# A hybrid encoder layer on one core: transfers in pieces and staged later, copies moved to GpSimd, q's norms from transposes

## The chip, the cores and the metric

The kernel is one program on one core of a Trainium2 chip. Its time is the device time from launch to end in microseconds (us). Every instruction belongs to an engine with its own in-order queue: PE is TensorE (matmuls and transposes; PEld its weight loads), DVE is VectorE, ACT is ScalarE, POOL is GpSimd, SP is SyncE, from whose queue all DMA transfers of this kernel are issued. An engine that waits for a semaphore holds up all that stands behind the waiting instruction in its own queue.

## The reference

One encoder layer over two sequences (1024 and 2048 tokens, model width 1024): an RMSNorm, one input projection, two parallel token mixers, a gated merge, an output projection and a residual. Branch A is neighbourhood attention with 8 heads of 64. Branch B is a bidirectional gated DeltaNet with 4 heads of 128, which is where most of the change sits. Cut to what matters here:

```python
proj = einsum('btd,de->bte', _rms_norm(x, norm_g), w_in)
qkv = silu(conv5(qkv_b)).reshape(B, T, 3, 4, 128)         # centred 5-tap conv
q = _l2_norm(qkv[:, :, 0]) * 128 ** -0.5                  # x * rsqrt(sum(x * x) + EPS)
k = _l2_norm(qkv[:, :, 1]);  v = qkv[:, :, 2]
# per direction, in chunks: a triangular solve, then a scan that carries S
sol = triangular_solve(a_mat, rhs, lower=True, unit_diagonal=True)
o_b = _rms_norm(o_fwd + o_bwd, dn_norm_g) * silu(z_b)
merged = sigmoid(gate_a) * (o_a @ w_branch_a) + sigmoid(gate_b) * (o_b @ w_branch_b)
y = x + merged @ w_out
```

## The kernel before

All float32 operands of the large products are split into a high and a low float16 part, and a product is three float16 matmuls (high by high, high by low, low by high).

**Stage 1, the function `deltanet`, from the start to about 1705 us.** The tokens stand in 12 half blocks of 256. The normalised input of each half block, transposed and split (`hh`, `hl`, 512 KB each), is written once to DRAM (`hdr`) and then fetched again for each of five rounds over the weights; there are two buffers of each, so half n is fetched when half n-2 has been let go. The projection's weights come in tiles of 1024x128 (`w`). For each tile, half a tile at a time (256 KB, `wst`, in the functions `staged`, `maximum` and `split_tile`), DVE takes the largest magnitude, a scale is made of it, and after a second fetch ACT and DVE make the high and the low part. Two such streams of weights run side by side, and the buffer `xt` has two places, one for each.

The order is written out by hand, in slots. `step_slot` issues one slot: it lets the generators of the chains (S), the inverses (I), the weights and rows (W, H), the operands (O) and the finishing steps (F) each go one step, and between these it fills PE with products of weights and halves until the slot holds 33.5 units (one unit is a float16 matmul of 256 columns). A generator that yields n is called again n slots on. `at(n, ...)` puts a call at the start of the n-th slot from now, `end(...)` at the end of this slot, after three quarters of its products. All five queues of this stage keep the order in which the code issued them. If the products run dry, transposes of the identity (`idle`) fill a slot to half.

The weights' steps stand in the middle of a slot:

```python
st = staged(src, k)          # DMA of a half tile
yield WD                     # WD = 1
amax(wm2[:, n, k:k + 1], st) # DVE
yield
```

So a half tile is issued in the middle of one slot, read by DVE in the middle of the next, and the next half tile is issued one slot later. `launch`, at a slot's start, fetches a half block with two transfers and hands it to the products two slots later.

For each head and each block of 512 tokens (24 in all) `operands` makes q, k and v from the convolution. q's norm: ACT squares q into the spent raw tile, PE multiplies the four squared 128x128 pieces by a column of ones (`pn`, float32, 8 columns), and DVE and POOL make the reciprocal root. `inverse` (12 in all) solves the triangular systems in 32x32 blocks: the blocks' inverses come back as `RR`, are copied into the diagonal of `P` (`u.E`, half of them by ACT, half by DVE) and, in `level1`, into the tile `Q64`, all of 32 partitions by 128 elements.

**Stage 2, to about 2384 us,** is the attention: slots of four tokens' tiles of projection (`ppn`) with the scores, the softmax and the values of earlier blocks. There PE, DVE and ACT keep the written order; DMAs and POOL are ordered by the framework's scheduler. Near its end `begin` starts a *chunk* (256 tokens of the merge): it loads `x` in two halves, attention's result `oad` and DeltaNet's `obd`, then `z` and the gates `th`; POOL multiplies `obd` by `z`, DVE takes the largest magnitude of `x`. `begin` takes six numbers: how many slots on the loads, the product on POOL and the four other steps come. `oad` of block 5 is written only shortly before by `block_out`.

**Stage 3** is the merge and the output projection.

## Time and profile before

| | |
|---|---|
| median of 3 runs | 2824.47 us (2822.04 to 2829.65) |
| the profiled execution | 2828.49 us, span 2826.7 us |
| mean granted clock of TensorE | 0.989 |
| busy: PE / DVE / ACT / POOL | 2705.9 / 1771.9 / 1398.1 / 899.6 us |

A row of the timeline or of the groups names the engine, the operation, `out<-in` by the program's tiles, the shape and how many; a bracket or the part behind the bar gives the time for which the engine stood idle just before, and what ended the wait. The granted clock is given as a share of 2.4 GHz: 1.00 is 2.4 GHz, 0.50 is 1.2 GHz. Matmuls overlap, so that a matmul's own duration is longer than its step: what it costs PE is the distance from its start to the next one's.

### The profile page before, as it was taken

How to read it: one execution, taken by the hardware profiler on the slowest of the kernel's cores; microseconds unless marked ns; L12 is line 12 of the kernel's file. 1: busy time of each engine (PE TensorE's matmuls, PEld its weight loads, DVE VectorE, ACT ScalarE, POOL GpSimd, SP SyncE). 2: the span in 40 equal slices, each digit the busy share in tenths (PEclk: the TensorE clock that was granted, in tenths of full speed). 3: DMA queues.
4: the chain of work that ended last, by engine and by line, in shares of the span. 5: the costliest groups of instructions: out<-in, count | busy, mean ns of one | idle time of the engine just before them, and what ended most of it. 6: DMA issues, size and time to landing. Idle time of an engine off the chain costs nothing. (4 is left out here: it accounts for less than half of the span.)

```text
span 2826.7 us, 65273 instructions
## 1 busy us (share of the span) xinstructions
PE 2705.9 (96%) x25140; PEld 2165.2 (77%) x25140; DVE 1771.9 (63%) x4266; ACT 1398.1 (49%) x3861; POOL 899.6 (32%) x1545
## 2 busy tenths in 40 slices
PE   7999999999999999999999999999999989999999
PEld 6888888978788977888888896666666657766675
DVE  7667766576675767747576522666666667555554
ACT  4455554555445555456454543666666755112211
POOL 2232120131112221112212215444444443555553
PEclk9999999999999999999999999999999999999999
DMA  8433442344533354322436737433332465443341
GB/s 255 152 112 94 122 116 81 105 139 124 125 99 99 112 145 119 90 88 88 131 103 172 201 118 209 132 105 95 94 102 86 140 200 204 165 164 130 134 147 68
DMA packets 488277, 365.00 MB, mean 129 GB/s; under 512 B 144291, under 2 KB 450847, under 8 KB 487071
## 3 DMA queue, kind: packets, MB, share of 16 engines
q1 hardware_dynamic: 487967, 360.84, 42.9%
q8 instruction: 198, 3.24, 0.5%
q14 instruction: 112, 0.92, 0.1%
HBM read 262.53 MB, written 98.20 MB: 128 GB/s over the span
## 5 line engine op out<-in xcount | busy, mean ns | idle before, releaser
L61 PE MATMUL pp<-hh,w 128*128 128x256 f16 x6912 | 1196.4, 275 | 8.7 <-DVE thz L61 3.9
L61 PEld LDWEIGHTS <-w 128*128 128x128 f16 x10368 | 1014.9, 99 | 135.1 <-issue 5.2
L61 PE MATMUL pp<-hl,w 128*128 128x256 f16 x3456 | 948.9, 275 | 0.6 <-DVE hl L61 0.6
L61 PEld LDWEIGHTS <-y 128*128 128x128 f16 x2304 | 224.8, 98 | 37.6 <-issue 9.4
L61 PE MATMUL ppn<-whi,rl 128*128 128x384 f16 x768 | 252.2, 328 | 0.0
L61 PE MATMUL ppn<-whi,rh 128*128 128x384 f16 x768 | 251.2, 327 | 0.0
L61 PE MATMUL ppn<-wlo,rh 128*128 128x384 f16 x768 | 251.2, 327 | 0.0
L61 POOL TENSOR_TENSOR th<-th 128x128 f32<-128x128 f32 (+1 forms) x240 | 153.8, 657 | 142.0 <-DVE th L61 129.2
L61 PEld LDWEIGHTS <-rh 128*128 128x128 f16 x1536 | 144.9, 98 | 69.6 <-issue 1.0
L61 ACT ACTIVATE thz<-pp,wfc 128x256 f32<-128x256 f32 x288 | 124.6, 472 | 148.5 <-PE pp L61 91.7
L61 PEld LDWEIGHTS <-mm 128*128 128x128 f16 x1008 | 98.7, 98 | 115.1
L61 ACT ACTIVATE mm<-th 128x256 f16<-128x256 f32 x144 | 59.1, 447 | 236.1 <-POOL th L61 231.8
L61 DVE TENSOR_TENSOR pl<-pT,ph 128x384 f16<-128x384 f32 (+1 forms) x192 | 110.9, 600 | 82.3 <-ACT ph L61 81.0
L61 DVE CUSTOM_DVE_ANT_0 Sb<-pS,bt 128x384 f32<-128x384 f32 (+1 forms) x192 | 108.9, 599 | 70.9 <-PE pS L61 30.6
L61 POOL TENSOR_TENSOR rqk<-rqk,mhalf 128x4 f32<-128x4 f32 x48 | 52.7, 1097 | 298.4 <-DVE rqk L61 295.1
L61 ACT ACTIVATE Sb<-Sb,nm,pq 128x384 f32<-128x384 f32 (+1 forms) x192 | 140.2, 734 | 0.7 <-DVE nm L61 0.7
L61 DVE TENSOR_REDUCE wm<-wst 128x1 f32<-128x512 f32 (+1 forms) x111 | 82.2, 762 | 79.0 <-DMA wst<-in_w_in 60.3
L61 ACT ACTIVATE vn<-pk,nbeg 128x128 f32<-128x128 f32 x176 | 64.8, 368 | 134.7 <-PE pk L61 133.9
L61 ACT ACTIVATE raw<-pp,wfc 128x256 f32<-128x256 f32 x144 | 63.6, 474 | 137.2 <-PE pp L61 135.2
L61 ACT ACTIVATE Os<-pon,rsn 128x64 f32<-128x64 f32 x192 | 49.9, 312 | 156.3 <-PE pon L61 156.2
L61 DVE SCALAR_TENSOR_TENSOR mm<-th,mm 128x256 f16<-128x256 f32 x144 | 80.6, 592 | 66.1 <-ACT mm L61 65.9
L61 PEld LDWEIGHTS <-rl 128*128 128x128 f16 x768 | 75.2, 98 | 60.1 <-issue 30.9
(621 smaller groups left out, 5614.6 us busy)
## 6 DMA issues: line engine op xcount, KB each, us to landing
wst<-in_w_in SPq DMA_DIRECT2D x124, 256.0 KB
gtd<-thz SPq DMA_DIRECT2D x192, 128.0 KB
hh<-hdr SPq DMA_DIRECT2D x48, 512.0 KB
hl<-hdr SPq DMA_DIRECT2D x48, 512.0 KB
th<-gtd SPq DMA_DIRECT2D x24, 1024.0 KB
vw<-vd SPq DMA_DIRECT2D x320, 64.0 KB
IT<-gd SPq DMA_DIRECT2D x48, 256.0 KB
bt<-ud SPq DMA_DIRECT2D x256, 48.0 KB
```

Of the source, the lines that this page charges most:

```text
L61: i = f(*a, **k)
```

## The change

Eight edits: (1) a half block is fetched in four transfers of 256 KB, one now, two in the next slot, one in the slot after, and handed over four slots later instead of two; (2) `WD` is 2 instead of 1, the half tiles of weights are issued at the end of the slot (`end`) and the trailing yields of `maximum` and `split_tile` are gone, so that a half tile still comes every second slot; (3) the steps that load the decay rows wait one slot more; (4) q's norm: PE transposes q (`ptq`), ACT squares the transposed tile out of PSUM, DVE sums over 128 elements; (5) 192 copies of 32x128 (half of `u.E`'s and all of `Q64`'s) go from DVE to POOL; (6) 28 identity transposes stand in the prologue; (7) a chunk loads `obd` and `z` ahead of `oad`; (8) the first chunk's `begin` stands one slot earlier, with its later steps in the same slots as before.

```diff
--- before.py
+++ after.py
@@ -265,7 +265,7 @@
             t.n = n
         wsc, wfc = (dcp.tile([128, NT + 5], F32, name=n) for n in ("wsc", "wfc"))
         wm2 = dcp.tile([128, NT + 20, 2], F32, name="wm2")
-        WD = 1
+        WD = 2
 
 
         c1 = dcp.tile([128, 8], F32, name="c1")
@@ -431,14 +431,13 @@
 
             n = src.shape[0] // 256
             st = wk.tile([128, n, src.shape[1]], F32, name="wst", tag="xt", bufs=2)
-            SY.dma_start(st, src[128 * n * k:128 * n * k + 128 * n].rearrange("(k p) c -> p k c", p=128))
+            end(SY.dma_start, st, src[128 * n * k:128 * n * k + 128 * n].rearrange("(k p) c -> p k c", p=128))
             return st
 
         def maximum(src, n, k):
             st = staged(src, k)
             yield WD
             amax(wm2[:, n, k:k + 1], st)
-            yield
 
         def split_tile(t, old, k):
 
@@ -455,7 +454,6 @@
             t.half += 1
             if t.half == 2:
                 at(1, setattr, t, "w", t.w_)
-            yield
 
 
         wba = [dcp.tile([128, 8, 16], F16, name=f"wba{i}") for i in range(2)]
@@ -603,7 +601,7 @@
                 for j, (a, b) in enumerate(((0, 1), (0, 0), (1, 0), (1, 1))):
                     r0, c0 = 256 * p + 128 * a, 512 * b + 128 * q
                     SY.dma_start(st[:, j], w_out[0][r0:r0 + 128, c0:c0 + 128])
-                yield 1 + WD
+                yield 2
                 hi, lo = (wk.tile([128, 7, 128], F16, name="wos", tag=t, bufs=2) for t in ("raw0", "raw2"))
                 S.activation(hi[:, 0:3], st[:, 1:4], AF.Identity, scale=so4)
                 end(low, lo[:, 0:3], st[:, 1:4], hi[:, 0:3])
@@ -870,7 +868,7 @@
                     yield
                 for d in range(2):
                     SY.dma_start(DT[:, d], tb.gd[4 * bi:4 * bi + 4, 4 * d + h, :][None, :, :].to_broadcast([128, 4, 128]))
-                yield 2
+                yield 3
                 for d in range(2):
                     G.tensor_tensor(DT[:, d], DT[:, d], mask[:, d, None, :].to_broadcast([128, 4, 128]), op=ADD)
                 yield
@@ -924,14 +922,15 @@
                 T.transpose(pt[:, c, :], o.kh[:, c, :], ident)
             S.activation(o.KQ[:, :, 0, :], pt, AF.Copy)
             cv.more(4)
-            S.activation(flat(rqt), qv, AF.Square)
-            yield
-            pn = ps_tr.tile([128, 4, 8], F32, name="pn", tag="tr")
+            yield
+            ptq = ps_tr.tile([128, 4, 128], F32, name="ptq", tag="tr")
             for c in range(4):
-                T.matmul(pn[:, c, :], flat(rqt)[:, c, :], ones, start=True, stop=True)
+                T.transpose(ptq[:, c, :], qv[:, c, :], ident)
             nq = wk.tile([128, 4], F32, name="rqk", bufs=4)
+            S.activation(flat(rqt), ptq, AF.Square)
             cv.silu()
-            end(rsq, nq, pn[:, :, 0])
+            end(V.tensor_reduce, nq, flat(rqt), AX.X, ADD)
+            end(rsq, nq, nq)
             done(0)
             yield
             G.tensor_scalar(o.rq, nq, 128.0 ** -0.5, 1.0, op0=MUL, op1=MUL)
@@ -1082,7 +1081,7 @@
                         if b % 2:
                             S.activation(u.E[sl(b), :, sl(b)], u.Pd[sl(b)], AF.Copy)
                         else:
-                            V.tensor_copy(u.E[sl(b), :, sl(b)], u.Pd[sl(b)])
+                            G.tensor_copy(u.E[sl(b), :, sl(b)], u.Pd[sl(b)])
             yield
 
             def level1(l, lv, Z):
@@ -1094,8 +1093,8 @@
 
                 for u in l:
                     ca, cb = 32 * u.qa - u.A, 32 * u.qb - u.A
-                    V.tensor_copy(Q64[sl(u.qa), :, ca:ca + 32], u.Qd[sl(u.qa)])
-                    V.tensor_copy(Q64[sl(u.qb), :, cb:cb + 32], u.Qd[sl(u.qb)])
+                    G.tensor_copy(Q64[sl(u.qa), :, ca:ca + 32], u.Qd[sl(u.qa)])
+                    G.tensor_copy(Q64[sl(u.qb), :, cb:cb + 32], u.Qd[sl(u.qb)])
 
             def level2(l, lv, Z):
                 for c in range(4):
@@ -1249,8 +1248,13 @@
                 n = l.pop(0)
                 t = half_tiles()
                 for i in range(2):
-                    SY.dma_start(t[i], hdr[n % 12 // 2][:, i, n % 2])
-                at(2, halves.__setitem__, n, t)
+                    for j in range(2):
+                        f = SY.dma_start, t[i][:, 4 * j:4 * j + 4], hdr[n % 12 // 2][:, i, n % 2, 4 * j:4 * j + 4]
+                        if i + j:
+                            at(i + j, *f)
+                        else:
+                            f[0](*f[1:])
+                at(4, halves.__setitem__, n, t)
             l = todo["op"]
             if l and len(live) < SLOTS and len(gens["H"]) + len(ahead) + len(live) < 6 + (len(rel) > 11) and opstage[0] and nraw.get(l[0], 0) == (6 if l[0][1] in LAST else 9) and \
                     len(tabs) > l[0][1] // 2:
@@ -1299,6 +1303,10 @@
         two(pt0[0], pt0[0].st)
         pts.append(transposed(xs[1], t0[0], 128))
         low_part(pts[1], *t0, 128)
+
+        t = ps_tr.tile([128, 4, 128], F32, name="idle", tag="tr")
+        for _ in range(28):
+            T.transpose(t[:, 0, :], ident, ident)
         sg = small()
         next(sg)
         amax(wm2[:, 1, 0:1], pt0[1].st)
@@ -1694,7 +1702,7 @@
             c.th = [big(f"th{h}", 4, 2, TB) for h in range(2)]
             op = big("op", 2, 2, 4, TB)
             c.o = [(op[:, j, 0], op[:, j, 1]) for j in range(2)]
-            for t, d in ((x[:, 0], oad), (x[:, 1], obd), (z, szd)):
+            for t, d in ((x[:, 1], obd), (z, szd), (x[:, 0], oad)):
                 SY.dma_start(t, d[i // 2].rearrange("(k p) t -> p k t", p=128)[:, :, cs])
             for h in range(2):
                 SY.dma_start(c.th[h].rearrange("p e j t -> p (e j) t"), gtd[i][8 * h:8 * h + 8].rearrange("e p t -> p e t"))
@@ -1926,8 +1934,8 @@
             if hp_ == 3 and b == 0:
                 branch_weights(0)
             for t in range(4):
-                if hp_ == 3 and b == 2 and t == 2:
-                    begin(order[0], (0, 3, 3, 4, 4, 5))
+                if hp_ == 3 and b == 2 and t == 1:
+                    begin(order[0], (0, 4, 4, 5, 5, 6))
                 mm = proj_mm(w, b, t)
                 slot(mm)
                 work(1, mm)
```

The order on SP around the fetch of one half block late in round two, before (`wst` are half tiles of weights, `hh` and `hl` the half block, `IT<-gd` the decay rows, `gtd`, `szd` and `zad` stores):

```order
370 L61 DMA ed_13745<-P 32x4x32 x8
371 L61 DMA IT<-gd_2717 128x4x128 x2
372 L61 DMA gtd_98<-thz 128x256
373 L61 DMA wst<-in_w_in 128x4x128 x2
374 L61 DMA gtd_98<-thz 128x256 x2
375 L61 DMA hh<-hdr_70 128x2048
376 L61 DMA hl<-hdr_70 128x2048
377 L61 DMA wst<-in_w_in 128x4x128 x2
```

The same half block on SP in the change:

```order
411 L61 DMA hh<-hdr_70 128x1024
412 L61 DMA hl<-hdr_70 128x1024
413 L61 DMA ed_13908<-P 32x4x32 x8
414 L61 DMA gtd_98<-thz 128x256
415 L61 DMA wst<-in_w_in 128x4x128 x2
416 L61 DMA hl<-hdr_70 128x1024
417 L61 DMA wst<-in_w_in 128x4x128 x2
418 L61 DMA gtd_98<-thz 128x256 x2
419 L61 DMA hh<-hdr_70 128x1024 x2
420 L61 DMA hl<-hdr_70 128x1024
421 L61 DMA wst<-in_w_in 128x4x128 x2
422 L61 DMA hl<-hdr_70 128x1024
```

The four pieces of a half block now stand apart, with half tiles of weights between them.

On DVE, the start of one inverse in the order before (`RR` are the blocks' inverses, `wm` the maxima of half tiles):

```order
1222 L61 STREAM_TRANSPOSE RR<-RR 128x512
1223 L61 COPY P<-RR 32x4x32 x8
1224 L61 TENSOR_REDUCE wm_141<-wst 128x1 x2
1225 L61 COPY Q_147<-RR 32x4x32 x4
1226 L61 SCALAR_TENSOR_TENSOR P<-raw_12664,cw,P 128x512
```

On POOL in the change, where such copies stand now, between the convolution's adds and the decay rows' adds (`IT<-IT,mask`):

```order
383 L61 COPY P<-RR 32x4x32 x8
384 L61 COPY Q_147<-RR 32x4x32 x4
385 L61 TENSOR_TENSOR Vt<-Vt,KQ 128x512
386 L61 TENSOR_TENSOR P<-P,KQ 128x512
387 L61 TENSOR_TENSOR IT<-IT,mask 128x512 x2
388 L61 COPY Q_147<-RR 32x4x32 x4
```

The twelve copies of the first half of an inverse have left DVE's queue and stand in POOL's; the four of the second half come behind the adds that wait for the decay rows.

On SP at the first chunk, before (`oad<-otn` is the write of attention's block 5, `vd` and `vw` attention's values):

```order
940 L61 DMA oad_23559<-otn 128x512
941 L61 DMA vw<-vd_28329 128x1x256 x3
942 L61 DMA vd_28329<-vt 128x256
943 L61 DMA x<-oad_23559 128x4x256
944 L61 DMA x<-obd_76 128x4x256
945 L61 DMA wst<-in_w_branch_b 128x4x128
946 L61 DMA z<-szd_88 128x4x256
947 L61 DMA th_33103<-gtd_99 128x8x256
```

And in the change:

```order
1005 L61 DMA x<-obd_76 128x4x256
1006 L61 DMA z<-szd_88 128x4x256
1007 L61 DMA th_33134<-gtd_99 128x8x256
1008 L61 DMA oad_23702<-otn 128x512
1009 L61 DMA wst<-in_w_branch_a 128x4x128
1010 L61 DMA th_33135<-gtd_99 128x8x256
1011 L61 DMA x<-oad_23702 128x4x256
```

`obd` and `z` now stand ahead of the write of `oad`, and only the load of `oad` stands behind it.

## Rows read from the trace of the kernel before

**Rows 1.** The page: busy time, share of the span and instructions of each engine.
```profile
PE 2705.9 (96%) x25140; PEld 2165.2 (77%) x25140; DVE 1771.9 (63%) x4266; ACT 1398.1 (49%) x3861; POOL 899.6 (32%) x1545
```

**Rows 2.** Windows, stages 1 and 2: width, each engine's busy time, clock, DMA share, GB/s.
```profile
30.00:1681.00 1651.00, 1577.97 (x16423) 1402.12 (x16422) 1080.49 (x2527) 860.41 (x2455) 347.39 (x602) 0.99 0.43 123
1706.00:2384.00 678.00, 653.19 (x5418) 435.36 (x5417) 428.16 (x1313) 433.38 (x1193) 317.12 (x637) 0.99 0.44 128
```

**Rows 3.** Waits of PE, then of DVE, in stage 1: us in total, times, longest.
```profile
PE lv L61 <- DVE Z L61: 11.2, 5, 4.9
...
DVE X L61 <- DMA YT<-ed: 30.6, 7, 7.0
```

**Rows 4.** Groups of DVE by shape: busy, mean ns, idle before and by whom.
```profile
L61 DVE TENSOR_REDUCE wm<-wst 128x1 f32<-128x512 f32 x94 | 61.7, 681 | 67.8 <-DMA wst<-in_w_in 49.2 <-DMA wst<-in_w_out 11.5 <-DMA wst<-in_w_branch_b 5.4
...
L61 DVE COPY Q<-RR 32x128 f32<-32x128 f32 x96 | 22.7, 236 | 1.5
```

**Rows 5.** Timeline, 997 to 1008 us, SP, DVE and PE: start, duration, instruction.
```profile
997.72 0.97 SPq L61 DMA_DIRECT2D wst<-in_w_in  x2
...
1001.53 0.66 SPq L61 DMA_DIRECT2D hh<-hdr  x1
...
1004.16 1.47 DVE L61 TENSOR_REDUCE wm<-wst 128x1 f32<-128x512 f32 x2 [6.04 <-DMA wst<-in_w_in]
...
1006.22 0.41 DVE L61 COPY Z<-lv 128x256 f32<-128x256 f32 x1
...
1006.78 1.12 PE L61 MATMUL lv<-P,Z 64*64 64x64 f32 x16 [4.85 <-DVE Z L61]
```

**Rows 6.** Timeline of PE: first and last of ten such waits.
```profile
477.10 0.39 PE L61 MATMUL lv<-P,Z 64*64 64x64 f32 x6 [2.10 <-DVE Z L61]
...
1376.75 0.51 PE L61 MATMUL pm<-ident,wma 128*128 128x128 f32 x3 [1.75 <-DVE wma L61]
```

**Rows 7.** Windows: five half-clock stretches of stage 1, the largest, then all five.
```profile
1005.21:1012.03 6.82, 5.25 (x36) 4.10 (x37) 6.72 (x16) 4.03 (x17) 1.11 (x2) 0.50 0.69 222
...
sum 20.43, PE 18.52 PEld 13.41 DVE 19.28 ACT 13.55 POOL 1.34; mean PE 3.71 PEld 2.68 DVE 3.86 ACT 2.71 POOL 0.27
```

**Rows 8.** Timeline of PE around q's sums and around a group of four transposes.
```profile
595.71 0.96 PE L61 MATMUL pn<-ones,raw 128*128 128x8 f32 x8
596.52 0.27 PE L61 MATMUL pp<-hh,w 128*128 128x256 f16 x1
...
603.87 0.63 PE L61 MATMUL ptv<-ident,P 128*128 128x128 f32 x4
604.34 0.27 PE L61 MATMUL pp<-hh,w 128*128 128x256 f16 x1
```

**Rows 9.** Timeline, 2258 to 2276 us: SP, POOL and PE at the first chunk.
```profile
2258.13 0.45 SPq L61 DMA_DIRECT2D oad<-otn  x1
...
2261.72 0.38 SPq L61 DMA_DIRECT2D x<-oad  x1
...
2263.24 0.50 SPq L61 DMA_DIRECT2D z<-szd  x1
...
2270.95 2.35 POOL L61 TENSOR_TENSOR x<-x,z 128x1024 f32<-128x1024 f32 x1 [6.69 <-DMA z<-szd]
...
2275.86 0.69 PE L61 MATMUL pqk<-ident,sqn 128*128 128x128 f32 x2 [5.99 <-POOL sqn L61]
```

**Rows 10.** Windows: the half-clock stretch at the first chunk.
```profile
2274.97:2281.79 6.82, 5.93 (x22) 2.56 (x23) 2.59 (x8) 0.75 (x2) 3.32 (x8) 0.50 0.34 99
```

**Rows 11.** Groups of POOL: a small copy, and the decay rows' adds.
```profile
L61 POOL COPY raw<-raw 128x2 f32<-128x2 f32 x96 | 17.5, 217 | 172.2 <-ACT raw L61 171.7
...
L61 POOL TENSOR_TENSOR IT<-IT,mask 128x512 f32<-128x512 f32 x48 | 60.9, 1284 | 75.0 <-DMA IT<-gd 69.9 <-PE idle L61 5.2
```

**Rows 12.** One tile's instructions: the copies into `Q64`, ns shortest/median/longest.
```profile
L61 DVE COPY Q<-RR x96: 204/218/1157, 268.4 to 1584.8; 32x128 f32<-32x128 f32 x96
```

**Rows 13.** Timeline of PE in the prologue, where the 28 transposes go.
```profile
20.25 0.47 PE L61 MATMUL pm<-ident,wma 128*128 128x128 f32 x1 [3.59 <-DVE wma L61]
```

## The prediction

> **What bounds the kernel now.** I read the page's busy times first: PE is busy for 2705.9 of 2826.7 us [rows 1], so the end moves by only two things, less work on PE or less waiting of PE. The windows by stage come next. In stage 1 PE is busy for 1577.97 of 1651 us, in stage 2 for 653.19 of 678 [rows 2]: 73 and 25 us stand open, and the merge behind has nearly nothing. Then the waits of PE, to see for whom it waits. In stage 1 the largest is for DVE's copy `Z`, 11.2 us in five waits [rows 3], though DVE is busy for only 1080 of 1651 us [rows 2]. So DVE is not too slow, it is late, and the groups of DVE tell why: before the maxima of half tiles of weights it stood idle for 67.8 us, 66 of these for the transfer `wst` [rows 4].
>
> One such chain, read forward in the timeline [rows 5]: SP issues two half tiles at 997.72; they land at 1004.16, 6.4 us later, with a half block of 1 MB (`hh`, `hl`) issued into them at 1001.53; DVE has nothing else it may do and waits 6.04 us; the copy `Z`, three instructions behind in its queue, comes at 1006.22; PE's `lv<-P,Z` needs it and had stood still for 4.85 us. I find ten waits of PE behind a late `wst` of this kind, from 477.10 us to 1376.75 us [rows 6], together 22 us. After five of them the records show PE's clock at 0.50, that is 1.2 GHz, for 20.43 us, in which PE was busy for 18.52 [rows 7]; at 2.4 GHz that work is done in half, so 9.3 us more belong to the same cause.
>
> **The change part by part.** *q's norm.* The step from the start of `pn` to the next matmul is 595.71 to 596.52, 0.81 us for four products; four transposes take 603.87 to 604.34, 0.47 us [rows 8]. There are 24 operand blocks: 24 x 0.34 = 8.2 us less work on PE, and all of it on the bounding engine. DVE gets 24 sums over 512 elements; the nearest row, a reduction of the same size, is 681 ns [rows 4]: 16 us on an engine with a third of stage 1 free. ACT's square is the same size as before, but it now stands behind PE's transposes of its own slot, and the tanh and the exponentials behind it wait with it; PE's own waits for ACT are small, so I put this with the new waits below.
>
> *The weights' transfers.* A unit on PE is about 0.12 us (0.47 / 4) [rows 8], a slot of 33.5 units 3.9 us. Before, a half tile is issued in the middle of one slot and read in the middle of the next: 3.9 us, less than the 6.4 us of rows 5. Now it is issued after three quarters of a slot and read in the middle of the second slot after: 1.75 slots, 6.9 us, 2.9 us more lead. Of the ten waits (the longest 4.85, 3.22 and 2.65) that leaves 1.95 and 0.3 us and takes 19.7 of 22 away, if each shrinks by the lead. The pieces of the half block act in the same direction, since the 1 MB that ran into rows 5 now comes as 256 KB, 512 KB and 256 KB in three slots. Against it stands that SP issues in order and may itself be late. Bounds: nothing, and all of 31.3 us (22 + 9.3). I take 0.7 of it, 22 us: the lead alone gives 0.9 of the waits, and I leave a fifth for late issues and for clock stretches that another wait brings on.
>
> *The first chunk.* SP may load `oad` only after its write, issued at 2258.13; the load goes out at 2261.72 and `z` behind it at 2263.24; POOL, in order, stands for `z` until 2270.95, and the norms of the projection stand behind that product on POOL, so PE waits 5.99 us for `sqn` [rows 9]. The clock is then at 0.50 for 6.82 us, 5.93 of them busy [rows 10]: 3.0 us. In the change `obd` and `z` are issued ahead of the write of `oad` and one slot earlier, so they have landed when POOL comes to them; the load of `oad` alone is late, and only DVE's maximum reads it, two slots on. I take the whole, 9.0 us; what is late next there is that maximum, with room. At the least it gives 4, if 2 MB of `z`, `obd` and `th` delay the write of `oad` and the values' loads behind it.
>
> *The copies.* Two kinds of 96, of one size, at 0.236 us [rows 4]: 45 us leave DVE, and with them the odd long one (median 218 ns, longest 1157) [rows 12]. On POOL the trace has no such copy. Its copy of 2 elements takes 0.217 us, its add of 512 elements 1.284 us [rows 11], so 192 cost 42 to 247 us; I take the lower end's neighbourhood, 0.3 us and 58 us, and POOL is busy for only 347 of 1651 us [rows 2]. What hides them: PE reads `Q64` two slots after the copies are issued (7.8 us) and the diagonal of `P` three slots after. Gone is that cover where POOL stands before the adds of the decay rows, for which it waited 69.9 us in all [rows 11]; the extra slot of edit 3 gives those 3.9 us more. The Trainium skill, GPSIMD Engine Reference, section 4.1, says that elementwise work belongs on VectorE and that GpSimd is about twice as slow with two inputs and near par with one; no row here shows a copy of this size on POOL. By the factor of two a copy takes 0.47 us, and the sum would be the same while POOL's free time hides it.
>
> *The prologue.* PE stands 3.59 us for a maximum at 20.25 [rows 13]; 28 transposes at 0.12 us are 3.3 us and fit into it at 2.4 GHz, and at 1.2 GHz hold the next product up by 3 us. Behind it PE waits for the next weights from DVE anyway. From 3 lost to 3 won; I take 1 won.
>
> *New waits.* ACT behind PE, POOL's queue, and slots in which the products run dry because a half block is handed over two slots later: a half block carries eight tiles of 24 matmuls, 192 x 0.12 = 23 us, against four slots of 15.6 us, so this holds except in the last rounds, where four tiles last 11.5 us. Between 0 and 14 us; I take 4.
>
> **The sum.** 8.2 + 22 + 9.0 + 1 - 4 = 36 us. The profiled execution took 2828.5 us, 2792.5 after; the median of the runs lies 4 us under it, so I forecast 2788 us. Its own bounds: all of the weights' 31.3, 3 from the prologue, no new waits and 5 from shorter waits for the inverses' transfers give 2768; a quarter of the weights' part, 4 from the chunk and 14 of new waits give about 2816.
>
> **The rivals.**
> *Another transfer takes the place.* DVE also waits 30.6 us for `X<-YT`, the inverses' blocks [rows 3], and that lead is not changed. If a DVE freed of one wait only meets the next, the weights' part gives 6 instead of 22: 2804. For it: the two lie near each other in the same queue. Against it: the ten waits of rows 6 follow `wst`, not these.
> *It does not do what it says.* With two places for two streams, a half tile's buffer is read by DVE in the very slot at whose end the next transfer is issued into it. If DVE is late, SP stands for it and holds stores and half blocks behind. Then the longer lead gives nothing and SP's hold costs some 5: 8 + 9 + 1 - 4 - 5 = 9 us, 2815.
> *POOL becomes what PE waits for.* The copies of an inverse's second half stand behind the decay rows' adds. If PE waits 2 us in each of 12 inverses, and half of these bring a half-clock stretch that costs 1.9 us (9.3 / 5), 35 us go: 2823. For it is the 69.9 us of rows 11, against it the two slots of cover. The Trainium skill's section named above speaks for this one; no row shows its price.
> *Slower: the half blocks come late.* There are two buffers, and half n is fetched only when half n-2 is let go. If its last piece, which SP issues two slots later than before and behind the weights, lands after the products want it, PE waits, say 1 us, and loses 1.9 us to the clock: 2.9 us for each half block. 44.5 us (the 36 and 8.5 more) are reached at 16 of the 48; at 24 it is 70 us, 2858. Against it: 23 us of products against 15.6 us.
>
> **How the numbers follow.** I give 0.60 to the forecast, 0.20 to the other transfer, 0.08 to the lead that gives nothing, 0.07 to POOL, 0.05 to the half blocks. The range is 2770 to 2814: it holds the forecast's own bounds but for their ends, and the first rival; the rest lies above. A measurement of this kernel can tell about 0.3%, 8.5 us, from no change, so faster means under 2816. Faster: 0.86 (the forecast, nearly all of the first rival, half of the second); the same: 0.09 (POOL, the other half); slower: 0.05.
>
> **What would show it.** The steps are right if DVE's idle time before `wm<-wst` falls from 67.8 to under 25 us, the half-clock stretches of stage 1 become fewer, PE shows no wait for `sqn` near the first chunk and POOL none for `z` there, and the step of `ptq` is 0.44 to 0.5 us. Wrong would be: `wst` waits as long as before, PE waits for `hl` or `hh` by DMA, or waits of `lv` for POOL. If PE's idle time in stage 1 stays near 73 us, the forecast fails with it.

## The result and the profile after

The changed kernel takes 2801.16 us (median of 4 runs, 2797.34 to 2805.1) beside 2824.16 us of the kernel before in the same session: ratio 0.9916, interval 0.9895 to 0.9936. That is 23 us less, inside the range of 2770 to 2814 us, and 13 us above the forecast of 2788. The profiled execution took 2802.75 us with a span of 2801.0, 25.7 us under the span before.

The page's busy times of the changed kernel, which answer to [rows 1]: PE is busy 11.6 us less and does 72 matmuls less, POOL is busy 62.9 us more.

```profile
PE 2694.3 (96%) x25068; PEld 2157.9 (77%) x25068; DVE 1767.1 (63%) x4098; ACT 1394.5 (50%) x3861; POOL 962.5 (34%) x1737
```

To see where the 25.7 us come from I cut both traces at the same places: 35 us, the first and the last product of stage 2. A row of this view has the window, its width, the busy times of PE, PEld, DVE, ACT and POOL, the granted clock, the DMA share and GB/s. First the kernel before, stages 1 and 2:

```profile
35.00:1705.46 1670.46, 1600.10 (x16626) 1423.62 (x16624) 1077.72 (x2529) 864.87 (x2481) 353.88 (x615) 0.99 0.43 123
1705.46:2379.51 674.05, 649.24 (x5381) 431.62 (x5379) 425.57 (x1307) 432.87 (x1191) 314.77 (x634) 0.99 0.44 128
```

The same two of the changed kernel:

```profile
35.00:1680.96 1645.96, 1587.64 (x16530) 1413.67 (x16528) 1061.56 (x2363) 861.17 (x2482) 423.49 (x807) 0.99 0.44 125
1680.96:2354.82 673.86, 648.90 (x5380) 431.84 (x5378) 426.61 (x1307) 433.09 (x1191) 315.47 (x633) 0.99 0.45 129
```

Stage 1 is 24.5 us shorter, stage 2 only 0.2. These 0.2 us hide two movements. Cut at the same product of both, the 2101st of the 2304 `ppn` (the last of them ends this view), stage 2 is 2.2 us longer up to there (539.92 us after 537.70), and the stretch behind, with the first chunk, is 2.2 us shorter; before, then after:

```profile
2243.16:2306.10 62.94, 55.98 (x432) 34.92 (x430) 37.51 (x116) 37.75 (x104) 26.44 (x52) 0.95 0.52 159
```

```profile
2220.88:2281.66 60.78, 56.54 (x431) 35.69 (x430) 39.27 (x115) 37.54 (x104) 27.31 (x51) 0.94 0.55 164
```

The longer first part is not the change's: over all kernels below it takes 534.2 to 542.8 us.

In stage 1 PE stands idle for 58.3 us (width less PE's busy time) where it was 70.4. The rest needs the clock. The sums over the stretches of stage 1 in which PE's clock was granted at 0.50 (1.2 GHz), before and then after:

```profile
sum 34.13, PE 32.06 PEld 23.53 DVE 26.46 ACT 22.06 POOL 4.84; mean PE 4.01 PEld 2.94 DVE 3.31 ACT 2.76 POOL 0.60
```

```profile
sum 27.89, PE 26.71 PEld 20.43 DVE 19.42 ACT 14.67 POOL 8.67; mean PE 3.34 PEld 2.55 DVE 2.43 ACT 1.83 POOL 1.08
```

Half of PE's busy time in these stretches is lost: 16.0 us before, 13.4 after. So of the 24.5 us between these two executions, 12.0 are waits of PE, 2.7 the clock, and 9.8 work of PE at full clock. I use these three numbers (waiting, half-clock loss, work) for every run below; how far one execution of a kernel can be trusted with them stands behind the table.

The groups of DVE that answer to [rows 4] and [rows 3] (busy, mean ns, idle before by whom), then POOL's that answer to [rows 11], and the two kinds of copies that are new there:

```profile
L61 DVE TENSOR_REDUCE wm<-wst 128x1 f32<-128x512 f32 x94 | 61.6, 678 | 29.0 <-DMA wst<-in_w_in 25.3 <-DMA wst<-in_w_branch_a 2.2 <-DMA wst<-in_w_out 0.3
L61 DVE COPY X<-YT 32x1024 f32<-32x1024 f32 x12 | 13.5, 1127 | 16.6 <-DMA YT<-ed 16.5
...
L61 POOL TENSOR_TENSOR IT<-IT,mask 128x512 f32<-128x512 f32 x48 | 61.2, 1295 | 4.9 <-DMA IT<-gd 4.9
L61 POOL COPY Q<-RR 32x128 f32<-32x128 f32 x96 | 38.4, 400 | 19.2 <-PE lv L61 14.7
L61 POOL COPY P<-RR 32x128 f32<-32x128 f32 x96 | 29.8, 310 | 68.3 <-DVE RR L61 54.6 <-DMA szd<-thz 10.1
```

DVE's wait for half tiles of this shape fell from 67.8 to 29.0 us (that for the 17 larger ones, 128x1024, rose from 11.2 to 18.4) and that for the inverses' blocks from 30.6 to 16.5; POOL's wait for the decay rows fell from 69.9 to 4.9. What PE waits for now in stage 1 (us in total, times, longest):

```profile
PE pt L61 <- DVE hl L61: 10.4, 7, 3.3
PE pp L61 <- DVE thz L61: 8.3, 5, 3.2
PE lv L61 <- ACT Q L61: 7.8, 6, 3.9
...
PE pp L61 <- DMA hl<-hdr: 5.0, 2, 2.7
```

The copy `Z` that led [rows 3] is gone from the head of the list, but other waits stand there, the late half block (`hl`) among them.

### The profile page after: what moved, and what is told of

It reads as the page before. It is cut to its first block, busy times and chain, and to the rows that moved or that the text cites. A ratio compares the mean times of both kernels' runs of the same rounds, so it can differ in the third digit from the quotient of the medians.

```text
span 2801.0 us, 65317 instructions
## 1 busy us (share of the span) xinstructions
PE 2694.3 (96%) x25068; PEld 2157.9 (77%) x25068; DVE 1767.1 (63%) x4098; ACT 1394.5 (50%) x3861; POOL 962.5 (34%) x1737
## 4 chain that ended last, share of the span: by engine, by line
PE 70%; DVE 11%; DMA 7%; ACT 4%; SPq 3%; issue 2%; POOL 2%; DVEq 0%; POOLq 0%; ACTq 0%
PE pp L61 29%; PE ppn L61 10%; PE pk L61 6%; SPq L61 3%; DVE YT L61 2%; PE pT L61 2%; PE pS L61 2%; DVE P L61 2%; PE lv L61 2%; PE pon L61 2%; DMA wst<-in_w_in 1%; DVE Yo L61 1%; PE gq L61 1%; DMA IT<-gd 1%; PE idle L61 1%
## 5 line engine op out<-in xcount | busy, mean ns | idle before, releaser
L61 POOL TENSOR_TENSOR th<-th 128x128 f32<-128x128 f32 (+1 forms) x240 | 147.5, 632 | 151.0 <-DVE th L61 138.0
L61 DVE SCALAR_TENSOR_TENSOR P<-raw,cw,P 128x512 f32<-128x512 f32 x144 | 115.5, 802 | 0.5
L61 DVE SCALAR_TENSOR_TENSOR S<-S,egl,pk 128x128 f32<-128x128 f32 x160 | 54.8, 342 | 94.5 <-PE pk L61 70.8
```

The source lines that it names most:

```text
L61: i = f(*a, **k)
```

## The experiments

All were timed in five rounds, each beside the kernel before on the same chip; rows compare by their ratios, since not all had the same one. Stage 1 of each, from 35 us to the first product of stage 2, cut as above; `put off` is how often the planner puts a step of the operands off, `idle transposes` those of stage 1 and, behind the plus, of the prologue, both counted in the order that the code writes:

| kernel | ratio (interval) | stage 1 | PE waiting | half-clock loss | work | put off | idle transposes |
|---|---|---|---|---|---|---|---|
| before | 1 | 1670.5 | 70.4 | 16.0 | 1584.1 | 96 | 188 |
| changed | 0.9916 (0.9895-0.9936) | 1646.0 | 58.3 | 13.4 | 1574.3 | 91 | 184+28 |
| e1 norm alone | 0.9997 (0.9985-1.0008) | 1667.2 | 67.7 | 21.7 | 1577.8 | 126 | 192 |
| e2 lead alone | 1.0052 (1.0034-1.007) | 1684.3 | 73.5 | 23.0 | 1587.8 | 106 | 216 |
| e3 copies alone | 1.0057 (1.0039-1.0076) | 1675.3 | 72.1 | 26.0 | 1577.2 | 91 | 136 |
| e4 chunk alone | 0.9983 (0.9968-0.9997) | 1676.6 | 68.9 | 25.1 | 1582.7 | 96 | 188 |
| e5 pieces alone | 0.9993 (0.9983-1.0003) | 1661.4 | 62.2 | 17.2 | 1582.0 | 100 | 176 |
| e6 lead and pieces | 1.0025 (1.0014-1.0037) | 1671.2 | 68.1 | 18.9 | 1584.2 | 92 | 187 |
| e8 prologue alone | 1.0038 (1.0026-1.0051) | 1682.1 | 74.5 | 23.7 | 1583.9 | 96 | 188+28 |
| e7 changed, whole halves | 0.9926 (0.991-0.9941) | 1649.8 | 62.4 | 16.1 | 1571.2 | 94 | 147+28 |
| e9 changed, chunk spread | 0.9892 (0.987-0.9914) | 1648.4 | 55.1 | 20.2 | 1573.1 | 91 | 184+28 |
| e10 changed, no prologue | 0.9889 (0.9866-0.9911) | 1645.0 | 54.2 | 18.8 | 1572.0 | 91 | 184 |
| e11 changed, copies on DVE | 1.0018 (1.0004-1.0031) | 1674.6 | 75.1 | 25.4 | 1574.1 | 103 | 172+28 |
| e12 the same, order held | 0.9909 (0.9894-0.9924) | 1645.3 | 58.5 | 11.4 | 1575.4 | 91 | 184+28 |

Each row is one profiled execution, and the executions of one kernel lie some us apart (17 of the kernel before, beside e9 to e11, from 2816.02 to 2834.55 us; e4's is the slowest of its 12). How far the columns go, the kernels tell in which PE has the same order in stage 1: the kernel before, e4 and e8 on one hand, the changed kernel, e9, e10 and e12 on the other. Within such a group the work agrees to 3.4 us, the waiting to 5.6 and the half-clock loss only to 9.0. Between the groups the work (1582.7 to 1584.1 us against 1572.0 to 1575.4) and the waiting (68.9 to 74.5 against 54.2 to 58.5) differ clearly, the half-clock loss (16.0 to 25.1 against 11.4 to 20.2) does not. So some 10 us of work and 12 to 15 of waiting are the change's, while the 2.7 us of clock between the two executions above are not shown to be.

The mean granted clock is known of every run, and (1 - clock) x span, averaged over a kernel's runs, is an estimate of what the clock costs it in the whole span: 27 to 29 us for the kernel before (four sessions), 29 for the changed one, 28 for e1, 36 for e2, 42 for e3, 35 for e8, 32 for e11, 24 for e12.

**One part of the change at a time, on the kernel before.** e1 has only the new norm, e2 only the weights' lead (`WD = 2`, the transfer at the slot's `end`, the trailing yields gone), e3 only the copies and the decay rows' slot, e4 only the first chunk:

```diff
# e1, 24 blocks
-            S.activation(flat(rqt), qv, AF.Square) ... T.matmul(pn[:, c, :], flat(rqt)[:, c, :], ones)
+            T.transpose(ptq[:, c, :], qv[:, c, :], ident) ... S.activation(flat(rqt), ptq, AF.Square)
# e2
-        WD = 1
+        WD = 2
# e3
-                yield 2
+                yield 3
-                    V.tensor_copy(Q64[...], u.Qd[...])
+                    G.tensor_copy(Q64[...], u.Qd[...])
# e4
-            for t, d in ((x[:, 0], oad), (x[:, 1], obd), (z, szd)):
+            for t, d in ((x[:, 1], obd), (z, szd), (x[:, 0], oad)):
```

Expected of e1:

> The kernel before with only the change of q's norm. Theory (the step of PE is the bound): 24 blocks x 0.34 us go, PE's busy time falls by about 8 us and the time by about 8 us (ratio 0.997), with PE idle in stage 1 near 70 us as before. Rival (ACT's square, now behind PE's transposes, holds up the tanh and the exponentials, or DVE's 24 sums come in the way): PE's busy time falls by the same 8 us, but PE's idle time in stage 1 rises by 5 us or more, and the time is within 3 us of before.

Expected of e2:

> The kernel before with only the longer lead of the weights' half tiles (read two slots after, issued at the end of a slot). Theory: DVE's idle time before the maxima of weights falls from 67.8 us to 25 to 35, as in the changed kernel, the PE waits behind a late half tile in stage 1 (22 us) shrink to under 6, and the time falls by 8 to 15 us. Rival (another transfer takes the place): DVE's idle time before the maxima falls as much, but DVE waits more for the inverses' blocks or PE waits for other late work, and the time falls by under 5 us.

Expected of e3:

> The kernel before with only the 192 small copies on POOL and the decay rows' adds one slot later. Theory: POOL's wait for the decay rows falls from 69.9 us to about 5, PE shows no new wait behind POOL, and the time is within 4 us of before. Rival (POOL is what PE waits for): PE waits of 1 us or more whose releaser is one of these copies, and the time rises by 5 us or more. Third (DVE's queue was what made PE late): the time falls by 5 us or more, because DVE comes earlier to the copies behind which PE stood.

Expected of e4:

> The kernel before with only the first chunk's loads one slot earlier and the load of oad last. Forecast of the prediction: 9 us less (PE's wait of 5.99 us for sqn and the half-clock stretch behind it go). What the changed kernel's trace suggests instead: the wait for sqn goes, but 3.5 MB of loads issued in a row put the half tiles of the branch weights late, ACT waits 5 us for one, PE waits 2 to 3 us behind ACT and its clock falls all the same: 0 to 4 us less.

*e1* took 2823.07 us beside 2823.44: nothing. Its work fell by 6.3 us and its waiting by 2.7, but its half-clock loss rose by 5.7 in these executions (over all runs the clock costs the two the same to about 1 us): neither the theory's 8 us of time nor the rival's waiting for ACT. *e2* took 2839.65, 16.2 us more, which neither expectation had. The rival's mechanism is what its trace shows. DVE's wait for half tiles fell as far as in the changed kernel, and the one behind it stayed:

```profile
L61 DVE TENSOR_REDUCE wm<-wst 128x1 f32<-128x512 f32 x94 | 60.8, 679 | 25.3 <-DMA wst<-in_w_in 21.6 <-DMA wst<-in_w_out 2.0 <-DMA wst<-in_w_branch_a 0.6
...
L61 DVE COPY X<-YT 32x1024 f32<-32x1024 f32 x12 | 14.7, 1225 | 32.5 <-DMA YT<-ed 32.4
```

Its longest wait of PE in stage 1 is one of these. In the timeline (start, duration, instruction, idle time before and its releaser) DVE stands 7.51 us for `YT`, and PE 5.53 us for the copy behind it:

```profile
1161.81 1.03 DVE L61 COPY X<-YT 32x1024 f32<-32x1024 f32 x1 [7.51 <-DMA YT<-ed]
1162.86 0.69 DVE L61 SCALAR_TENSOR_TENSOR P<-raw,P 128x512 f32<-128x512 f32 x1
```

```profile
1163.70 0.66 PE L61 MATMUL ptk<-ident,P 128*128 128x128 f32 x2 [5.53 <-DVE P L61]
```

So 42.5 us less waiting of DVE for half tiles (67.8 to 25.3) bought PE nothing: its waiting rose by 3.1 us, the half-clock loss by 7.0 and the work by 3.7, of which 28 idle transposes at 0.12 us are 3.4 (by the estimate above the clock costs it 9 us more over all runs). *e3* took 2840.22, 16.8 us more, and yet no wait of PE in its stage 1 has a POOL copy as its releaser: the rival's time without its mechanism. By the estimate above the clock costs it 15 us more than the kernel before, which is nearly all; why it costs more there is not shown. *e4* took 2816.92 beside 2823.44, 6.5 us less (0.8 to 9 by the interval): the sign of the forecast, and the mechanism that I had read from the changed kernel, 0 to 4 us, only in the lower half of what was measured. In its profile (an execution of 2832.2 us, above that median) SP stands 6.0 us for the write of `oad`, ACT 5.50 us for a half tile, and PE 2.44 us for ACT's `qs` where it had waited 5.99 for `sqn`; the stretch with the chunk, cut as above, takes 59.5 us where it took 62.9.

**The half blocks and the prologue.** e5 has the pieces alone, e6 the lead and the pieces, e7 is the changed kernel with whole half blocks, e8 the kernel before with the 28 transposes:

```diff
# e5, e6: pieces; e7: the other way
-                    SY.dma_start(t[i], hdr[n % 12 // 2][:, i, n % 2])
-                at(2, halves.__setitem__, n, t)
+                    for j in range(2): ... t[i][:, 4 * j:4 * j + 4] ... at(i + j, *f)
+                at(4, halves.__setitem__, n, t)
# e8
+        for _ in range(28):
+            T.transpose(t[:, 0, :], ident, ident)
```

> The kernel before with only the half blocks in four pieces, handed over two slots later. Theory A (a half block's 1 MB stands in front of every other transfer, so the pieces are what shortens all waits for transfers): DVE's waits for the weights' half tiles and for the inverses' blocks, 67.8 and 30.6 us before, both fall by a third or more, and the time falls by 10 to 20 us. Theory B (the pieces only move the wait to PE, which then waits for the late half block): waits of PE for hl or hh appear, 2 us or more each, and the time is within 5 us of before or over it.

> The kernel before with the longer lead of the half tiles (+16 us alone) and the half blocks in pieces. If the two need each other (a half tile that is issued at a slot's end lands in front of the next half block's first piece only when that piece is small): the time falls by 15 us or more against before, more than either alone. If they only add up: about 16 us more than with the pieces alone.

> The changed kernel with the half blocks whole again, as two transfers of 512 KB handed over after two slots. Theory A (the pieces carry the gain): 2815 to 2835 us, DVE's wait for the inverses' blocks back from 16.5 to about 30 us. Theory B (the pieces carry nothing): 2795 to 2803 us, with the two PE waits for hl gone.

> The kernel before with only the 28 transposes of the identity in the prologue. By the sum of the prediction: 1 us less, from 3 lost to 3 won. Rival (the moments at which PE's clock falls are a matter of how a wait of PE lies to what ran ahead of it, and any shift of the start deals them anew): the products, waits and transfers of stage 1 are as before, but the half-clock stretches lie elsewhere and the time moves by 4 us or more in either direction.

*e5*: 2821.88 beside 2824.26, which the measurement can't tell from none. DVE's wait for the inverses' blocks fell from 30.6 to 6.5 us, as theory A has it, but its wait for half tiles of both shapes only from 79.0 to 58.8, and PE waits once for `hl`, 2.2 us, as theory B has it. The profiled execution has 8.2 us less waiting of PE in stage 1; the median of the runs shows a quarter of that. *e6*: 2829.27, 5.0 more; the two singles add up to 13.8 more, so they help each other a little, but don't give the 15 us less. *e7*: 2802.89, theory B: inside the changed kernel the pieces carry nothing, the two waits for `hl` are gone, and DVE waits 10.6 us for the inverses' blocks, less than with the pieces.

*e8* needs the most care. After the prologue its instructions are those of the kernel before, in the same order, about 3 us later. It took 2836.22 beside 2824.26, 12 us more, where 28 transposes are 3.3 us of work: in stage 1 PE waits 4.1 us more and loses 7.7 more to the clock, and over all runs the clock costs it 7 us more than the kernel before. The same wait of PE, in both kernels 2.22 us long and before the same product, first before and then e8:

```profile
91.88 0.27 PE L61 MATMUL pp<-hh,w 128*128 128x256 f16 x1 [2.22 <-DVE thz L61]
```

```profile
95.08 0.27 PE L61 MATMUL pp<-hh,w 128*128 128x256 f16 x1 [2.22 <-DVE thz L61]
```

The windows of the 3.4 us just behind it, before and then e8: the clock is 1.00 in one and 0.50 in the other, and PE starts 32 matmuls or 18.

```profile
92.50:95.90 3.40, 3.40 (x32) 2.98 (x32) 3.40 (x6) 0.00 (x0) 0.42 (x1) 1.00 0.11 39
```

```profile
95.72:99.13 3.41, 3.41 (x18) 2.49 (x18) 3.41 (x6) 0.00 (x0) 0.40 (x1) 0.50 0.11 38
```

It is tempting to put this down to the start 3 us later. e4 says that no shift is needed. Its program is that of the kernel before until the first chunk, and in its profiled execution the same product comes at 91.83 us, 0.05 us from where it came before, behind the same wait; there too the clock falls:

```profile
91.83 0.27 PE L61 MATMUL pp<-hh,w 128*128 128x256 f16 x1 [2.21 <-DVE thz L61]
```

```profile
92.94:96.36 3.42, 3.42 (x18) 2.45 (x17) 3.38 (x8) 0.16 (x1) 0.00 (x0) 0.50 0.03 10
```

So whether the clock falls behind this wait differs between two executions of the same instructions. The 12 us of e8 are shown by its runs, but not that the shift is their cause.

**The changed kernel with one part otherwise.** e9 spreads the first chunk's loads, e10 leaves the prologue's transposes out, e11 puts the copies back on DVE:

```diff
# e9: obd and z at once; oad, th[0], th[1] one slot apart each
-                    begin(order[0], (0, 4, 4, 5, 5, 6))
+                    begin(order[0], (0, 4, 4, 5, 5, 6), (1, 2, 3))
# e10
-        for _ in range(28):
-            T.transpose(t[:, 0, :], ident, ident)
# e11
-                    G.tensor_copy(Q64[...], u.Qd[...])
+                    V.tensor_copy(Q64[...], u.Qd[...])
```

> The changed kernel with the first chunk's loads spread over four slots: obd and z first as now, oad one slot on, when its write is done, and the two halves of th one and two slots behind that. Theory (in the changed kernel SP stands 5 us for the write of oad behind 2.5 MB of loads, the half tile of the branch weights lands late, ACT waits 5.4 us for it, and PE 2.4 us for ACT's qs): these three waits go, the half-clock stretch at 2247 goes with them, and the time falls by 3 to 6 us, 2795 to 2798. Rival (something else, the products' evictions or DVE, is late there just behind): SP's and ACT's waits go, PE waits as long for another engine within 20 us, and the time stays within 2 us of the changed kernel.

> The changed kernel without the 28 transposes of the identity in the prologue. They cost 12 us when put into the kernel before, though 3.3 us of work at most. Theory (no price of their own: a shift of the start by one us deals the waits and half-clock stretches of stage 1 anew): the time moves by anything from -12 to +12 us, its loss in stage 1 at other places than in the changed kernel. Rival (they do cost 12 us, because PE's clock or the weights are late behind them): 2789 us, 12 less.

> The changed kernel with the 192 small copies back on DVE; the decay rows keep their later slot. If the copies on POOL cost 17 us as they did alone: 2784 us. If they carry part of the gain in this company (DVE comes earlier to what PE waits for): 2806 to 2820 us, with DVE's idle time before the weights' maxima lower and PE's waits for DVE longer. If neither: 2795 to 2805.

The chunk in the changed kernel first. SP issues `z`, the first `th`, the write of `oad`, the half tile of the branch weights and the second `th`, then stands 5.2 us (the view of SP's waits) until the write is done:

```profile
2234.14 0.50 SPq L61 DMA_DIRECT2D z<-szd  x1
2234.69 0.69 SPq L61 DMA_DIRECT2D th<-gtd  x1
2235.82 1.26 SPq L61 DMA_DIRECT2D oad<-otn  x1
2237.12 0.74 SPq L61 DMA_DIRECT2D wst<-in_w_branch_a  x1
2237.91 1.89 SPq L61 DMA_DIRECT2D th<-gtd  x1
2245.07 0.36 SPq L61 DMA_DIRECT2D x<-oad  x1
```

```profile
SPq L61 <- DMA oad<-otn: 5.2, 1, 5.2
```

The half tile, issued between two loads of 1 MB, can be read 8.8 us later; ACT stands 5.43 us for it with `qs` behind, and PE waits for `qs`:

```profile
2245.88 0.72 ACT L61 ACTIVATE y<-wst,abp 128x512 f16<-128x512 f32 x1 [5.43 <-DMA wst<-in_w_branch_a]
2246.51 0.47 ACT L61 ACTIVATE qs<-ppn 128x384 f32<-128x384 f32 x1
```

```profile
2247.03 0.32 PE L61 MATMUL ppn<-whi,rh 128*128 128x384 f16 x1 [2.38 <-ACT qs L61]
```

In e9 the load of `oad` is no longer waited for (SP's wait for its write is gone from that view), ACT's wait for the same half tile is 1.26 us, PE's wait for `qs` is gone (it stands 0.99 us for `sqn` instead), and the stretch with the chunk takes 57.57 us where the changed kernel takes 60.78:

```profile
2243.38 0.72 ACT L61 ACTIVATE y<-wst,abp 128x512 f16<-128x512 f32 x1 [1.26 <-DMA wst<-in_w_branch_a]
```

```profile
2223.14:2280.71 57.57, 53.53 (x431) 34.03 (x430) 38.84 (x114) 37.09 (x103) 26.89 (x51) 1.00 0.58 173
```

It took 2796.76 us beside 2824.89, ratio 0.9892: the theory's time, and the waits that it named are gone, but its interval overlaps that of the changed kernel, and the gain can't be credited to the spread loads. e10 and e11 have the changed kernel's loads and all three waits (PE stands 1.83 and 1.45 us for `qs`), and they pass the same stretch in 58.48 and 57.17 us, without a fall of the clock; e11's:

```profile
2247.46:2304.63 57.17, 53.66 (x432) 34.12 (x430) 38.94 (x114) 37.02 (x103) 26.86 (x52) 1.00 0.59 175
```

*e10*: 2793.38, ratio 0.9889, some 8 us under the changed kernel by the medians, overlapping too. Its stage 1 is as long as the changed kernel's to 1 us, and most of the difference between the two executions lies in stage 2, which the transposes don't touch; in e8 it lay in stage 1. That fits no price of their own, but they have no gain to show either. e9 and e10 have the lowest medians that were measured.

*e11*: 2829.22 beside 2824.89, ratio 1.0018: the whole gain gone, 28 us lost by putting back the part that alone cost 17. The code says how a copy can do that. The planner advances the operands' steps only while DVE's and ACT's counted cost of the slot is under 3000, and a copy on DVE counts 100 and its width, one on POOL nothing:

```python
if x[0] <= sn and (most is None or max(V.cost, S.cost) < most):
```

With the copies counted, a step is put off 103 times instead of 91, and from there on every queue has another order. On PE the two traces part behind the same `lv`, the changed kernel first:

```profile
630.14 0.45 PE L61 MATMUL lv<-RR,P 32*32 32x32 f32 x32
630.52 0.66 PE L61 MATMUL ptk<-ident,P 128*128 128x128 f32 x4
```

```profile
633.76 0.45 PE L61 MATMUL lv<-RR,P 32*32 32x32 f32 x32
634.15 0.39 PE L61 MATMUL pp<-hh,w 128*128 128x256 f16 x2
```

So e12 keeps the copies on DVE and takes them out of the count, by which PE, ACT and SP have the changed kernel's very order:

```diff
+    def free_copy(out, in_):
+        v = V.cost; V.tensor_copy(out, in_); V.cost = v
-                    G.tensor_copy(Q64[...], u.Qd[...])
+                    free_copy(Q64[...], u.Qd[...])
```

> The changed kernel with the 192 copies on DVE, but left out of the cost that the planner counts for DVE, so that PE, ACT and SP get the very order of the changed kernel (with the copies back on DVE and counted, 2829 us, the planner put off other steps and PE's order differed from there on). Theory (the order of the steps is what moved the 28 us, the engine of the copies little): 2797 to 2806 us. Rival (DVE's time is what counts: 45 us of copies stand ahead of what PE waits for): 2815 to 2830 us, with longer PE waits for DVE than in the changed kernel.

*e12*: 2799.82 beside 2826.49, ratio 0.9909, as fast as the changed kernel and in the theory's range. Stage 1 of e11, then of e12: DVE is busy for 1107.63 and 1105.58 us, the same, and PE waits 75.1 and 58.5.

```profile
35.00:1709.62 1674.62, 1599.49 (x16517) 1418.12 (x16516) 1107.63 (x2555) 861.31 (x2481) 356.08 (x615) 0.98 0.43 122
```

```profile
35.00:1680.27 1645.27, 1586.78 (x16531) 1413.17 (x16532) 1105.58 (x2556) 862.03 (x2484) 359.23 (x615) 0.99 0.44 125
```

Of the 16.6 us between these, 9 are two kinds of waits for transfers. e11's are these, where e12 has 2.7 us for `hl` and none for `RR<-rd`:

```profile
PE pp L61 <- DMA hl<-hdr: 6.2, 1, 6.2
PE lv L61 <- DMA RR<-rd: 5.5, 3, 3.2
```

DVE's own wait for half tiles is no guide to this: 18.4 us in e11, less than in e12 (26.6) or the changed kernel (29.0). With e11 beside it, e12 settles the part of the copies in the changed kernel: the engine that makes them is worth nothing that can be measured, the order that their counted cost sets is worth some 28 us. On the kernel before the same test was not made, so whether e3's 17 us are its order or POOL's time is open.

## Why the prediction was right, and where it was wrong

The sum gave 26.2 us for stage 1 (8.2 + 22 - 4), and 24.5 came; it gave 9.0 for the first chunk, and 2.2 came there, 0.2 in stage 2 as a whole. The 8.8 us between 9.0 and 0.2 (6.8 that the chunk lacks, 2.0 of scatter ahead of it) are most of what lies between the span's forecast fall of 36 and its fall of 25.7.

- **The step that failed is the first chunk** ("I take the whole, 9.0 us"). The wait of 5.99 us for `sqn` went, as forecast, but 2.38 us for `qs` took its place, and the clock is at 0.50 for 6.8 us there as before. `z` had not landed either when POOL came to it: POOL still stands 4.26 us, where 6.69 were before and the signs asked for none.

```profile
2240.21 2.71 POOL L61 TENSOR_TENSOR x<-x,z 128x1024 f32<-128x1024 f32 x1 [4.26 <-DMA z<-szd]
```

  Nor was the write of `oad` what made `z` late before: SP waited for it 0.5 us there, and 5.2 only in the changed kernel. I had asked only for whom the late loads were late and not what the earlier ones would now stand in front of: 3.5 MB issued within 12 us, with the branch weights' half tile between them. The bound of 4 us named the right cause and the wrong victims. Over the kernels the stretch with the chunk takes 61.6 to 63.0 us with the loads as before and 57.2 to 60.8 with them earlier, so the edits are worth 1 to 6 us, not 9; e4's runs (6.5, from 0.8 to 9) agree.
- **q's norm** was sized rightly as work. In the changed kernel a group of `ptq` takes 284.82 to 285.32, 0.50 us against 0.81 [rows 8], in the range given: 24 x 0.31 = 7.5 us.

```profile
284.82 0.66 PE L61 MATMUL ptq<-ident,KQ 128*128 128x128 f32 x4
285.32 0.27 PE L61 MATMUL pp<-hh,w 128*128 128x256 f16 x1
```

  In the table the kernels with the new norm have 1571 to 1578 us of work in stage 1, those without it 1582 to 1588, but for e3 with its 52 idle transposes less. Why alone it gave no time (e1) is not shown; its 24 sums on DVE count in the plan too, 126 steps were put off instead of 96, and so the order is another.
- **The weights' transfers.** In the changed kernel four waits of PE go back to a late `wst`, from 59.34 (3.29) to 1499.72 (1.42), 9.3 us together, where ten had 22 [rows 6]: 12.7 us less. With the 2.7 of the clock, which one pair of executions can't show, that is half of the 31.3, without it 0.4, and not 0.7. Other waits grew meanwhile (`lv` for ACT's `Q` from 0.7 to 7.8 us), so that PE's waiting fell by 12.0 in all. DVE's wait fell to 29.0 us, short of the "under 25", and the half-clock stretches behind 35 us did not become fewer: eight before, eight after. And e2 shows that this can't be credited to the lead alone: there the same fall went with 16 us more, and DVE met the inverses' blocks, which is the first rival's mechanism. In the changed kernel the two long waits of PE for `thz` go back to such a block too, as the one at 677.86 us:

```profile
673.65 1.05 DVE L61 COPY X<-YT 32x1024 f32<-32x1024 f32 x1 [4.60 <-DMA YT<-ed]
...
677.86 0.37 PE L61 MATMUL pp<-hh,w 128*128 128x256 f16 x1 [3.18 <-DVE thz L61]
```

- **The copies** cost POOL 68 us, where I took 58; PE has no wait for them, so the cover was read rightly and the POOL rival fell. The Trainium skill, GPSIMD Engine Reference, section 4.1, has work with one input at roughly the same rate on POOL as on VectorE; here a copy of 32x128 takes 0.400 and 0.310 us on POOL against 0.236 and 0.217 on DVE, 1.4 to 1.7 times as long, and the measurement decides. The section's factor of two, which the prediction put on a copy, is given there for two inputs; a copy has one. What I missed is that a planner counts them.
- **The late half blocks**, the rival on the other side, did occur: PE waits twice for `hl`, at 626.55 and 992.64, 2.72 and 2.25 us, each near a half-clock stretch or a late half tile, not 16 times. The four slots of cover hold nearly everywhere.
- **The prologue** was no gain of 1 us: 12 us lost alone, and by the medians some 8 less without it in the changed kernel, which the intervals don't tell from none.
- **The chances** were added up wrongly: by the terms named, faster is at most 0.60 + 0.20 + 0.04 = 0.84, the same 0.11, slower 0.05. The outcome, some 0.8% less, was on the likeliest side either way.

The gravest fault lies under all steps. The sum took the parts as independent. The six parts, each alone, changed the median by -0.4, +16.2, +16.8, -6.5, -2.4 and +12.0 us, together +35.7 (the decay rows' slot counted with the copies); together in one kernel they gave -23. Only the work behaves like a sum: without the idle transposes, at 0.12 us each, the six parts change it by -9.2 us together and the changed kernel by -9.3, closer than executions agree. Waiting belongs to one order and one set of arrival times, the half-clock loss to one execution besides, and every part but the chunk's and the prologue's changed the order of stage 1. That stage 1 came out within 2 us of its forecast is thus partly luck.

What stays open: which of the moved steps saves the 17 us of waiting between e11 and e12, and why each part alone falls so far from its term. It wasn't tried to move them one by one, nor to take the lead or the norm out of the changed kernel.

## What to carry to other kernels

Where a planner decides by counted costs, moving an instruction to another engine is two changes, one of time and one of order; hold the order fixed (as e12 does) before crediting the engine. Add up the work of the bounding engine, but give waits and clock as a range for the whole order, and learn how far that range goes from several executions of the same order before a difference in one trace is explained. Before moving loads earlier, list what is issued between and behind them, down to the small transfer that another engine stands for.

## What the runs showed of the hardware

- A wait of PE of the same length, before the same product, was followed by PE's clock at half in one execution and at full in another (2.22 us at 91.88 in the kernel before, 2.21 at 91.83 in e4), with the same instructions ahead. The half-clock loss of that same stage 1 was 16.0 and 25.1 us.
- At the chunk, behind the same loads, PE waited 1.45 (e11), 1.83 (e10), 2.10 (e7), 2.38 (changed), 2.44 (e4) and 2.63 us (e12) for the same `qs`; the clock was at half there for 0, 0, 3.4, 6.8, 6.8 and 6.8 us.
- A half tile of 256 KB that was issued between two loads of 1 MB could be read 8.8 us after its issue.
- Three of four small copies in a row took 1.09 to 1.18 us on DVE at 632.61 us in e11, where the median of the 96 is 0.218: even a short copy can have such an outlier.
